# The output projection by pairs of tiles with seven part products, as the first part of the stream

## The chip, the cores and the metric

The kernel runs on one core of a Trainium2 chip. The metric is the device time of one execution in microseconds (us), the median of several runs. The core has a matmul engine (PE, with its weight loads, PEld), a vector engine (DVE), a scalar engine (ACT), a small general engine (POOL), and queues that move data between its memories (DMA); all DMA of this kernel is issued by the sync engine (SP). Each engine works through its instructions in program order and waits at an instruction until what it needs is there.

## The reference

One layer of an encoder over 2048 tokens of width 1024, all in f32:

```
xn = rms_norm(x, ln_mix_g)
proj = xn @ w_in
y_a = mlstm_group(proj[...])              # bidirectional, 4 heads x 128
y_b = mla_group(proj[...])                # attention, 4 heads x 128
h = x + concat([y_a, y_b]) @ w_out        # the output projection, 1024 x 1024
h = h + conv_gated_mlp(rms_norm(h, ln_ffn_g), w_up, conv_w, conv_b, w_down)
gate = sigmoid(rms_norm(h, ple_norm_g) @ w_ple_gate)
h = h + gate * rms_norm(p @ w_ple_proj, ple_post_g)
return rms_norm(h, final_g)
```

## The kernel before

**Split matmuls.** Each f32 operand is split into a high part (ACT casts it) and a low part (DVE subtracts the high part from it); a product is three matmul passes, low x high, high x low, high x high. The helper `split` does this, on lines 118 and 121 of the profile (120 and 123 after the change), for all parts of the kernel, so the tile's name tells them apart: `pt` are the transposed weights of attention, `wo` the weights of the projection, `yhl` its input, `op` the operands of the stream's right side and `fw`/`fwd` those of its left side.

**Stages.** The input projection; then attention with the mLSTM work beside it (a string of letters, `order`, gives what each of 64 attention tiles (head, 128 queries) issues, and at each "." in it `pump` issues a share of the mLSTM steps, which `SIDE` sets); then `out_proj`; then `up_down`, called the stream below.

**The output projection.** For each of 16 token tiles: `load_y` loads the tile's y, DVE scales its attention half by the softmax sums (`rb`), `split`; two halves of 512 columns, each 8 k-parts x 3 passes = 24 matmuls of 128x512 (`out_mm`, PE line 131, into `bk`); DVE adds the result to x (line 1143); the sum is stored (`h1_d`), squared on ACT (1064), turned into a factor on POOL (139, 141) and scaled in place by DVE (1066). The eight transposes of a tile (1075) stand one tile late, and ACT copies them to a tile that is stored to `x2_d`. The weights are loaded as eight `wor` and split to `wo0`..`wo7`, four of them beside the last attention head.

**The stream.** Products of matrices of 2x2 blocks by seven part products instead of eight. A pair is two tiles of 128 rows; for each, `prod` issues four k-parts x 3 passes = 12 matmuls into one of four banks (x and y in `fxy`, z in `fz`, and a spare one `fs`), in the order A11 x B11, S1 x T1, A22 x T4 of the pair before, S2 x T2, A12 x B21, S4 x B22 of the pair before, S3 x T3. S1 to S4 are sums of the left side, formed by DVE in `up_prep` one pair ahead. B.. are blocks of the right side and T1 to T4 sums of them; `sums`, `wsums` and `gsums` form the T ahead of time and store them, and `load_op` loads and splits a block's operands, four pieces of 128x512 for each of seven operands, through a ring of raw places (tags t0, t1, ...; `orot`). The first block of 22 pairs does the up projection of the first half of the tokens with x2 as its right side; then come the other half, three blocks of the down projection, and the gate. In the stream before, the first up block's B11, T1 and T2 are formed in place by `sums` inside `out_proj`, its other operands are loaded in pairs 0 and 1, and these two pairs take results over by other additions ("not seeded").

**Tile places.** Every tile has a place named by a tag (w0.., x0.., t0.., u0..). A new tile in a place waits until all readers of the old one are done. PSUM banks come from pools: `sc` (scores, also `bk`), `tr`, `pv`, `ml` up to the projection, `fa` and `fb` for the stream.

Of the kernel before, what the change touches and what calls it, by code (L numbers as in the profile page):

```python
# [10 lines left out]
F32 = mybir.dt.float32  # L11
# [26 lines left out]
SIDE = 617  # L38
# [22 lines left out]
class Block:  # L61
# [4 lines left out]
    def __init__(self, ctx, tc, d):  # L66
# [13 lines left out]
        self.gt = self.cst.tile([P, 16, 16], F32, name="gt")  # L80
        dt = self.dram.tile
# [14 lines left out]
        self.x2_d = dt([P, KT, S], F32, name="x2_d")  # L96
        self.t_d = dt([2, 4, P, 4, 512], F32, name="t_d")
# [50 lines left out]
    def run(self, out):  # L148
# [807 lines left out]
    def attend(self, side):  # L956
# [58 lines left out]
        cur, self.wo = self.first, []  # L1015
        pts, pend = [], None
        for i, (h, qt) in enumerate(seq):
# [35 lines left out]
            cur = nxt  # L1053
        pv(pend, 1)
        sums(1)
        for _ in side:
            pass


    def norm_load(self, h, g, ssq_junk):  # L1060

        nc = self.nc
        ssq = self.stat(1, "nt_s")
        nc.scalar.activation(ssq_junk, h, AF.Square, accum_out=ssq)
# [3 lines left out]
    def transpose_out(self, xn, otag, dst):
        nc = self.nc
        pt = (self.tbank(), self.tbank())  # L1070
        xo = self.at(otag, [P, KT, P], name="nt_o")
        for f in range(2):
            for j in range(4):
                kt = f * 4 + j
                nc.tensor.transpose(pt[f][:, j, :], xn[:, kt * P:(kt + 1) * P], self.ident)
            nc.scalar.copy(xo[:, f * 4:f * 4 + 4], pt[f])
        nc.sync.dma_start(dst, xo)

    def load_wo(self, k):
        nc = self.nc  # L1080
        raw = self.at(("w13", "w13", "w13", "w13", "w13", "w12", "u2", "w0")[k], [P, D], name="wor")
        nc.sync.dma_start(raw, self.d["w_out"][0, k * P:(k + 1) * P, :] if k < 4 else self.wo_d[k - 4])
        w = self.at(f"x{(0, 1, 2, 3, 6, 7, 4, 5)[k]}", [P, 2, D], F32R, f"wo{k}")
        self.split(raw, w[:, 0], w[:, 1])
        self.wo.append(w)

    def load_y(self, c):
        yr = self.at(f"w{5 + c % 2}", [P, 8, P], name="yr")
        self.nc.sync.dma_start(yr, self.y_d[c])
        rb = self.row_bcast(self.at(f"u{c % 2}", [P, 512], name="rb"), self.ri_d[c].rearrange("h t -> (h t)"), 512)  # L1090
        ya = yr[:, 4:8].rearrange("p h t -> p (h t)")
        self.nc.vector.tensor_tensor(ya, ya, rb, op=ALU.mult)
        if c:
            y = self.at(f"x{10 + c % 2}", [P, 2, 8, P], F32R, "yhl")
            self.split(yr, y[:, 0], y[:, 1])
            return y[:, :, 0:4], y[:, :, 4:8]
        ys = []
        for f in range(2):
            ys.append(self.at(("w4", "w9")[f], [P, 2, 4, P], F32R, "yhl"))
            self.split(yr[:, 4 * f:4 * f + 4], ys[f][:, 0], ys[f][:, 1])  # L1100
        return ys
# [776 lines left out]
```

## Time and profile before

| | us |
|---|---|
| median of 3 runs | 2957.03 (2951.71 to 2958.16) |
| the profiled execution | 2961.99, of which span 2960.2 |
| PE busy | 2895.7 (98% of the span), 14738 matmuls and transposes |
| weight loads (PEld) busy | 2437.3 (82%) |
| DVE busy | 1991.5 (67%) |
| ACT busy | 1476.6 (50%) |
| last score matmul of attention ends | 1226.4 |
| first matmul of the stream | 1443.8 |

The span is the time from the first to the last instruction on the core. Busy times overlap between engines. The projection lies between the two last rows, some 217 us.

### The profile page before, as it was taken

The page shows a single profiled execution, that of the slowest core. Times are in us where ns is not written, and L with a number is a line of the kernel's source. Part 1 is how long each engine was busy: PE and PEld are TensorE (multiplying, and loading weights), DVE is VectorE, ACT ScalarE, POOL GpSimd, SP SyncE. Part 2 cuts the span into 40 slices and gives each one's busy share as a digit, 9 for nine tenths or more (in the row PEclk, how much of TensorE's full clock was granted, in tenths as well). Part 3 has the DMA queues.
Part 4 walks back from the last instruction along what each step waited for, and adds up shares of the span by engine and source line. Part 5 has one row for each costly group of instructions (what it writes and reads, how often), then busy time and mean ns, then how long its engine had stood idle before and what let it go on. Part 6 is the DMA issues. An engine that isn't in the chain of part 4 may idle for free.

```text
span 2960.2 us, 40962 instructions
## 1 busy us (share of the span) xinstructions
PE 2895.7 (98%) x14738; PEld 2437.3 (82%) x14738; DVE 1991.5 (67%) x3677; ACT 1476.6 (50%) x2883; POOL 145.9 (5%) x278
## 2 busy tenths in 40 slices
PE   8999999999999999999999999999999999999998
PEld 7888888888888888888788888788887788878776
DVE  7521555777777777635677877767777767676776
ACT  7311544656665666523455555655556333244654
POOL 3100000000000000000000000000000000001111
PEclk9999999999999999999999999999999999999999
DMA  6612444443333333457734554657776757585864
GB/s 186 128 57 95 146 132 153 120 146 98 103 100 100 98 118 114 145 178 256 243 137 164 190 172 147 206 177 234 233 228 201 231 180 246 167 261 196 277 195 157
DMA packets 396253, 496.93 MB, mean 168 GB/s; under 512 B 32385, under 2 KB 265361, under 8 KB 396049
## 3 DMA queue, kind: packets, MB, share of 16 engines
q1 hardware_dynamic: 396048, 494.31, 52.4%
q8 instruction: 116, 1.90, 0.3%
q14 instruction: 89, 0.72, 0.1%
HBM read 318.39 MB, written 175.83 MB: 167 GB/s over the span
## 4 chain that ended last, share of the span: by engine, by line
PE 46%; DMA 4%; DVE 4%; issue 2%; ACT 2%; POOL 1%; SPq 0%; POOLq 0%; ACTq 0%; DVEq 0%
PE fxy L1427 30%; PE fz L1427 11%; PE bk L131 4%; PE fs L131 1%; DMA tsum<-x_d 1%; DMA opr<-tw_d 1%; DMA opr<-in_w_ple_gate 1%; DVE pj L1756 0%; DVE fw L121 0%; ACT junk L1770 0%; DMA opr<-t_d 0%; DVE hb L1757 0%; ACT fw L118 0%; DMA t_d<-tsum 0%; ACT op L118 0%
## 5 line engine op out<-in xcount | busy, mean ns | idle before, releaser
L1427 PE MATMUL fxy<-op,fw 128*128 128x512 f32 x3552 | 857.7, 393 | 15.3 <-DVE fh L1413 5.4
L1427 PEld LDWEIGHTS fxy<-op,fw 128*128 128x128 f32 x3552 | 662.6, 189 | 174.2 <-ACT ug L1580 13.6
L1427 PE MATMUL fz<-op,fw 128*128 128x512 f32 x1776 | 440.0, 390 | 3.2 <-DVE xt L1143 2.1
L1427 PEld LDWEIGHTS fz<-op,fw 128*128 128x128 f32 x1776 | 332.0, 188 | 72.4 <-DVE xt L1143 2.4
L131 PE MATMUL bk<-wsp,xh 128*128 128x512 f32 (+1 forms) x768 | 234.5, 386 | 0.0
L118 ACT CAST pt<-tb 128x512 fp32r<-128x512 f32 x256 | 147.1, 587 | 174.9 <-PE tb L972 174.2
L914 DVE TENSOR_REDUCE mx<-bk 128x1 f32<-128x512 f32 x256 | 175.2, 685 | 65.8 <-PE bk L913 61.6
L1427 PE MATMUL fxy<-op,fwd 128*128 128x512 f32 x888 | 215.3, 390 | 0.2 <-DVE fh L1413 0.2
L131 PE MATMUL ppv<-pt,kv 128*128 128x256 f32 x1536 | 203.9, 287 | 0.0
L121 DVE TENSOR_TENSOR pt<-tb,pt 128x512 fp32r<-128x512 f32 x256 | 174.2, 686 | 38.0 <-ACT pt L118 36.6
L1427 PEld LDWEIGHTS fxy<-op,fwd 128*128 128x128 f32 x888 | 165.9, 188 | 35.3 <-DVE fh L1413 1.0
L932 ACT ACTIVATE pe<-bk,nm 128x512 f32<-128x512 f32 x256 | 174.6, 696 | 32.8 <-DVE nm L926 27.1
L131 PEld LDWEIGHTS ppv<-pt,kv 128*128 128x128 f32 x1536 | 189.0, 191 | 0.5 <-ACT pt L118 0.4
L131 PE MATMUL bk<-wo,yhl 128*128 128x512 f32 x744 | 177.1, 396 | 5.2 <-DVE yhl L121 5.2
L131 PEld LDWEIGHTS bk<-wo,yhl 128*128 128x128 f32 x744 | 139.9, 190 | 34.3 <-DVE yhl L121 5.6
L131 PEld LDWEIGHTS bk<-wsp,xh 128*128 128x128 f32 x768 | 145.6, 190 | 25.2
L131 PE MATMUL bk<-wsp,xl 128*128 128x512 f32 (+1 forms) x384 | 150.9, 393 | 8.1 <-DVE xl L121 8.1
L131 PE MATMUL bk<-xh,wqk 128*128 128x512 f32 x480 | 157.4, 393 | 0.0
L972 PE MATMUL tb<-ident,pe 128*128 128x128 f32 x1024 | 150.0, 273 | 3.7 <-DVE pt L121 3.7
L972 PEld LDWEIGHTS tb<-ident,pe 128*128 128x128 f32 x1024 | 121.9, 140 | 22.6 <-DVE pt L121 5.3
L118 ACT CAST fw<-hraw 128x1024 fp32r<-128x1024 f32 (+1 forms) x72 | 70.2, 981 | 125.5 <-PE fxy L1427 96.3
L121 DVE TENSOR_TENSOR fw<-fwr,fw 128x1024 fp32r<-128x1024 f32 x88 | 107.4, 1221 | 31.7 <-ACT fw L118 31.7
(348 smaller groups left out, 4806.9 us busy)
## 6 DMA issues: line engine op xcount, KB each, us to landing
fwr<-in_w_up SPq DMA_DIRECT2D x66, 512.0 KB, 4.7
fh<-h_d SPq DMA_DIRECT2D x48, 512.0 KB, 4.2
h_d<-fh SPq DMA_DIRECT2D x48, 512.0 KB, 4.0
s_d<-fwr SPq DMA_DIRECT2D x44, 512.0 KB, 2.6
fws<-s_d SPq DMA_DIRECT2D x44, 512.0 KB, 4.0
rw<-row_d SPq DMA_DIRECT2D x32, 512.0 KB, 4.9
tw_d<-tsum SPq DMA_DIRECT2D x60, 256.0 KB, 5.1
opr<-tw_d SPq DMA_DIRECT2D x60, 256.0 KB, 5.2
```

Of the source, the lines that this page charges most:

```text
L118: nc.scalar.copy(hi, src)
L121: (sub or nc.vector).tensor_tensor(lo, src, _f(hi), op=ALU.subtract)
L131: mm = lambda *a, **k: self.nc.tensor.matmul(*a, **k, skip_group_check=more)
L914: nc.vector.tensor_reduce(s.mx[:, kb:kb + 1], ps, axis=AX.X, op=ALU.max)
L932: nc.scalar.activation(s.pe[:, kb % 2], s.banks[kb], AF.Exp, bias=s.nm, scale=ASCALE, accum_out=s.rs[:, kb:kb + 1])
L972: nc.tensor.transpose(t[:, j, :], s.p[kb][:, j * P:(j + 1) * P], self.ident)
L1427: nc.tensor.matmul(out, a[:, k * P:(k + 1) * P], parts[lo], start=first, stop=lo == 1 and k == last, skip_group_check=more)
```

## The change

The output projection becomes eight pairs, numbered -8 to -1, at the head of the stream, with w_out as the right side and y as the left. Its weights' four sums per k-part are formed by `osums` beside attention (tiles 6 to 21) and stored to `to_d`. At the end of attention, all seven operands of the new block are loaded by `load_op(0, ...)`, with four raw places (`RAWS`). `up_prep` is cut in two (`prep_a`, `prep_b`) so that pair -8 can be prepared in two steps; the mLSTM steps end three tiles before attention's end. The class `Out` loads y (w12, w13, one buffer) and x, stores the result, and does the norm and the transposes of the tiles between products of later pairs. `sums(0)` now stores all four sums, and the first up block's operands are loaded at pair -1 as those of every other block. In the last pair of the gate stage, S4 x B22 of the pair before comes earlier. `out_proj`, `load_wo`, `load_y`, `out_mm`, `norm_load`, `transpose_out` and `turn` are gone. The rest of the diff renumbers blocks and gives tiles other places.

```
-SIDE = 617
+SIDE = 668
...
         self.attend(tail(self.mlstm()))
-        self.out_proj()
+        left.close()
+        pools(left, "left", ("fa", 2))
         right.close()
-        pools(right, "right", ("fa", 2))
-        left.close()
-        pools(left, "left", ("fb", 2))
-        self.up_down(out)
+        pools(right, "right", ("fb", 2))
+        self.stream(out)
...
         for i, (h, qt) in enumerate(seq):
-            if h == NH - 1 and qt in (4, 6, 8, 10):
-                self.load_wo(qt // 2 - 2)
+            if 6 <= i < 22 and i % 2 == 0:
+                next(osums)
...
-            if i == len(seq) - 2:
-                self.y0 = self.load_y(0)
+            if i == last - 3:
+                for _ in side:
+                    pass
+                self.load_op(0, "B11")
+                o.load(-8)
+            if i == last - 2:
+                self.load_op(0, "T1")
+                self.prep_a(-8)
+                o.load_x(-8, 0)
...
-            if nxt is None:
-                self.ps0 = self.pml.tile([P, 512], F32, name="wo0", tag="ml")
-                self.out_mm(self.ps0, self.y0, range(4), slice(0, 512))
...
+            if i == last - 1:
+                for n in ("T2", "B21", "T3"):
+                    self.load_op(0, n)
+                    if n == "T2":
+                        self.prep_b(-8)
         pv(pend, 1)
         sums(1)
-        for _ in side:
-            pass
+        self.load_op(0, "T4")
+        self.load_op(0, "B22")
...
+    def osums(self):
+        tt = self.nc.vector.tensor_tensor
+        L, H = slice(0, SB), slice(SB, 2 * SB)
+        for k in range(4):
+            a, b = [self.at(f"u{i}", [P, D], name="wos") for i in range(2)]
+            self.nc.sync.dma_start(a, self.d["w_out"][0, k * P:(k + 1) * P, :])
+            self.nc.sync.dma_start(b, self.wo_d[k])
+            yield
+            tt(a[:, H], a[:, H], a[:, L], op=ALU.subtract)
+            tt(b[:, H], b[:, H], a[:, H], op=ALU.subtract)
+            tt(a[:, L], b[:, H], a[:, L], op=ALU.subtract)
+            tt(b[:, L], b[:, L], b[:, H], op=ALU.subtract)
+            for i, t in enumerate((a[:, H], b[:, H], a[:, L], b[:, L])):
+                self.nc.sync.dma_start(self.to_d[i, :, k], t)
+            yield
...
+    RAWS = {(0, "B11"): range(4), (1, "B11"): (0, 1, 2, 3, 6, 7), (1, "T4"): range(4), (2, "B11"): range(6),
+            (4, "B11"): range(8), (6, "B11"): (0, 1, 2, 3, 4, 5, 7), (6, "T4"): (0, 1, 3)}
...
+    BLOCKS = ((-8, 8, 4), (0, NC2, 4), (NC2, NC2, 4), (2 * NC2, 8, 4), (2 * NC2 + 8, 8, 4), (2 * NC2 + 16, 8, 3),
...
+class Out:
...
+    def done(self, s, e):
+        b, nc, t = self.b, self.nc, s.o[e]
+        nc.sync.dma_start(b.h1_d[2 * s.pr + e], t)
+        ssq = b.stat(2, "nt_s")
+        for f in range(2):
+            nc.scalar.activation(b.at("s2", [P, SB], BF16, "junk"), t[:, f * SB:f * SB + SB], AF.Square,
+                                 accum_out=ssq[:, f:f + 1])
+        s1 = b.stat(1, "nt_t")
+        nc.gpsimd.tensor_tensor(s1, ssq[:, 0:1], ssq[:, 1:2], op=ALU.add)
+        self.norm[2 * s.pr + e] = t, b.rsq(s1, 1, 1.0 / D)
...
+    def beside(self, s, at, bank):
...
+        c = 2 * i + 12 if at < 4 else 2 * i + 15
+        if at in (1, 2, 5, 6) and 0 <= c < NT:
+            self.turn(c, at - 1 if at < 4 else at - 5, bank)
+        c = 2 * i + 15 if at == 4 else 2 * i + 14
+        if at in (4, 7) and 0 <= c < NT:
+            self.scaled(c)
...
+        if (i, at) == (-3, 3):
+            self.sums = b.sums(0)
+        if (i, at) in ((-3, 4), (-3, 6), (-3, 7), (-2, 2), (-2, 3), (-2, 5), (-2, 6), (-1, 1)):
+            next(self.sums)
...
-            if prev:
+            if prev and i < n - 1:
                 rest_z(prev)
```

The first place is the end of attention on ACT. `pe` are the exponentials of a tile (four banks), `pt` the casts of its transposes, `ya` a copy of its result. Before, from the first exponential of the last tile on, with `hy` of the mLSTM and the projection's first operands:

```order
L932 ACTIVATE pe,rs<-bk,nm 128x512
L118 CAST pt<-tb 128x4x128 x2
L932 ACTIVATE pe,rs<-bk,nm 128x512 x2
L868 ACTIVATE hy,dsq<-hy 128x128 x2
L988 COPY ya<-ppv 128x256
L932 ACTIVATE pe,rs<-bk,nm 128x512
L118 CAST yhl<-yr 128x512
L118 CAST pt<-tb 128x4x128
L868 ACTIVATE hy,dsq<-hy 128x128
L118 CAST pt<-tb 128x4x128
L118 CAST wo_13226<-wor 128x1024
L868 ACTIVATE hy,dsq<-hy 128x128
```

The same place after:

```order
L120 CAST fwd<-yr 128x512
L120 CAST op<-opr 128x512
L933 ACTIVATE pe,rs<-bk,nm 128x512
L120 CAST op<-opr 128x512
L989 COPY ya<-ppv 128x256
L120 CAST op<-opr 128x512 x2
L933 ACTIVATE pe,rs<-bk,nm 128x512 x2
L120 CAST op<-opr 128x512
L120 CAST pt<-tb 128x4x128
L933 ACTIVATE pe,rs<-bk,nm 128x512
L120 CAST pt<-tb 128x4x128
L120 CAST op<-opr 128x512 x2
```

The casts `op<-opr` of the new block's operands now stand between the four exponentials and between the casts of the transposes; before, these places held `hy` pieces and splits of `wo`.

The second place is the start of the projection, on DVE, from the splits of the last tile's transposes to the first addition of a product to x (`xt`). Before:

```order
L121 TENSOR_TENSOR pt<-tb,pt 128x4x128 x2
L121 TENSOR_TENSOR wo_13226<-wor,wo_13226 128x1024
L871 SCALAR_TENSOR_TENSOR hy<-hy,rsr,og 128x128 x4
L121 TENSOR_TENSOR wo_13231<-wor,wo_13231 128x1024
L121 TENSOR_TENSOR pt<-tb,pt 128x4x128 x2
L1092 TENSOR_TENSOR yr<-yr,rb 128x512
L121 TENSOR_TENSOR wo_13236<-wor,wo_13236 128x1024
L1467 MEMSET uv 128x2
L121 TENSOR_TENSOR wo_13241<-wor,wo_13241 128x1024
L121 TENSOR_TENSOR yhl<-yr,yhl 128x1024
L1511 TENSOR_SCALAR gt<-gt 128x8
L1143 TENSOR_TENSOR xt<-xt,wo_13099 128x512
```

The same place after, with the first addition on line 1346 (the S2 result of pair -8):

```order
L123 TENSOR_TENSOR pt<-tb,pt 128x4x128
L123 TENSOR_TENSOR op<-opr,op 128x512 x2
L123 TENSOR_TENSOR pt<-tb,pt 128x4x128 x2
L123 TENSOR_TENSOR op<-opr,op 128x512 x4
L123 TENSOR_TENSOR fw_13463<-yr,fw_13463 128x1024
L123 TENSOR_TENSOR op<-opr,op 128x512 x3
L123 TENSOR_TENSOR fw_13455<-yr,fw_13455 128x1024
L123 TENSOR_TENSOR op<-opr,op 128x512
L1336 TENSOR_TENSOR yr<-yr 128x512
L123 TENSOR_TENSOR op<-opr,op 128x512 x3
L1436 TENSOR_SCALAR gt<-gt 128x8
L1346 TENSOR_TENSOR xt<-xt,fxy 128x512
```

The first addition stands behind eleven more operand splits and two splits of pair -7 (`fw`). On PE the products of that stretch stand so after the change; `fw_12988` and `fw_12989` hold A11 and A12 of pair -8, `fw_12997`/`fw_12998` S1, `fw_13218`/`fw_13219` S2, and `fw_13455` A11 of pair -7:

```order
L1011 MATMUL tb<-ident,gt 32x128
L1361 MATMUL fxy<-op,fw_12989 128x512 x3
L1361 MATMUL fxy<-op,fw_12988 128x512 x4
L1361 MATMUL fz<-op,fw_12997 128x512 x4
L1361 MATMUL fz<-op,fw_12998 128x512 x4
L1361 MATMUL fz<-op,fw_12997 128x512 x4
L1361 MATMUL fxy<-op,fw_13218 128x512 x4
L1361 MATMUL fxy<-op,fw_13219 128x512 x4
L1361 MATMUL fxy<-op,fw_13218 128x512 x4
L1361 MATMUL fxy<-op,fw_13455 128x512 x10
L1361 MATMUL fxy<-op,fw_12988 128x512 x4
L1361 MATMUL fxy<-op,fw_12989 128x512 x4
```

A12 x B21 (the second row group of `fw_12988`) comes ten matmuls behind S2 x T2, with no other work of pair -8 between them; before, PE had the rest of tile 0's part products there.

The third place is the middle of the projection on DVE. Before, one tile and the next (line 1092 is the scaling of y, 1143 the addition, 1066 the norm's scaling):

```order
L1092 TENSOR_TENSOR yr<-yr,rb 128x512
L1143 TENSOR_TENSOR xt<-xt,bk 128x512 x2
L121 TENSOR_TENSOR yhl<-yr,yhl 128x1024
L1066 SCALAR_TENSOR_TENSOR xt<-xt,rsr,g_13246 128x1024
L1092 TENSOR_TENSOR yr<-yr,rb 128x512
L1143 TENSOR_TENSOR xt<-xt,bk 128x512 x2
L121 TENSOR_TENSOR yhl<-yr,yhl 128x1024
L1066 SCALAR_TENSOR_TENSOR xt<-xt,rsr,g_13246 128x1024
```

After, half a pair, from the addition of A12 x B21's result (1582 is the scaling of y, 1346 an addition, 1610 the norm's scaling in two halves):

```order
L1346 TENSOR_TENSOR xt<-xt,fxy 128x512
L123 TENSOR_TENSOR fw_13782<-yr,fw_13781 128x1024
L1346 TENSOR_TENSOR xt<-xt,fz 128x512
L123 TENSOR_TENSOR fw_13776<-yr,fw_13775 128x1024
L1346 TENSOR_TENSOR xt<-xt,fxy 128x512
L1582 TENSOR_TENSOR yr<-yr,rb 128x512
L1346 TENSOR_TENSOR xt<-xt,fz 128x512
L1610 SCALAR_TENSOR_TENSOR xt<-xt,rsr,g_13414 128x512
L1610 SCALAR_TENSOR_TENSOR xt<-xt,rsr,g_13416 128x512
L123 TENSOR_TENSOR fw_13956<-yr,fw_13955 128x1024
```

The scaling of a y that has just been loaded now stands ahead of the norm's scaling of the even tile of the pair before, whose transposes follow in the next pair.

## Rows read from the trace of the kernel before

**Rows 1.** The page: busy time, share of the span, instructions, by engine.

```profile
PE 2895.7 (98%) x14738; PEld 2437.3 (82%) x14738; DVE 1991.5 (67%) x3677; ACT 1476.6 (50%) x2883; POOL 145.9 (5%) x278
```

**Rows 2.** PE's waits (total us, times, longest) in 520:1230 and in 1520:2960.

```profile
PE tb L972 <- DVE pt L121: 3.7, 11, 0.5
...
PE fxy L1427 <- DVE fh L1413: 5.5, 5, 2.1
PE fxy L1427 <- ACT c L1576: 5.1, 6, 1.9
PE fxy L1427 <- ACT ug L1580: 4.8, 2, 2.6
```

**Rows 3.** PE's timeline: start, us, instructions, [idle before <- what ended it].

```profile
1226.01 0.40 PE L913 MATMUL bk<-kv,q_s 128*128 128x512 f32 x1
...
1237.71 5.88 PE L131 MATMUL ppv<-pt,kv 128*128 128x256 f32 x47
...
1247.82 0.66 PE L876 MATMUL mb<-ident,hy 128*128 128x128 f32 x4 [0.40 <-DVE xt L1143]
...
1257.13 13.66 PE L131 MATMUL bk<-wo,yhl 128*128 128x512 f32 x48 [5.21 <-DVE yhl L121]
...
1417.07 1.06 PE L1075 MATMUL tb<-ident,xt 128*128 128x128 f32 x8 [2.65 <-DVE xt L1066]
...
1443.83 2.79 PE L1427 MATMUL fz<-op,fw 128*128 128x512 f32 x11 [2.14 <-DVE xt L1143]
```

**Rows 4.** The chain that ended last, in 1225:1300: start, us, what.

```profile
1271.66 10.90 PE bk L131 x48
1282.56 0.87 PE tb L1075 x8
```

**Rows 5.** Windows: busy us (instructions) of each engine, granted clock, DMA share, GB/s.

```profile
520.00:1226.00 706.00, 691.92 (x4685) 621.67 (x4684) 515.83 (x1336) 431.28 (x1161) 44.54 (x62) 1.00 0.35 109
...
1250.00:1260.00 10.00, 4.79 (x16) 3.56 (x15) 4.50 (x5) 2.08 (x3) 0.74 (x2) 0.78 0.83 274
```

**Rows 6.** The chain that ended last, behind PE's last product.

```profile
2950.58 0.74 DVE pj L1756
```

**Rows 7.** Tile opr: the two instructions of a split, ns min/median/max.

```profile
L118 ACT CAST op<-opr x137: 602/618/628, 1436.1 to 2787.4; 128x512 fp32r<-128x512 f32 x137
L121 DVE TENSOR_TENSOR op<-opr,op x137: 682/686/694, 1436.7 to 2789.0; 128x512 fp32r<-128x512 f32 x137
```

**Rows 8.** Operand loads (line 1302) in 1400:1470, then ACT's and DVE's timeline there.

```profile
DMA to landing us min/median/max: 4.3/4.5/5.8
...
1441.84 1.20 ACT L118 CAST op<-opr 128x512 fp32r<-128x512 f32 x2 [2.52 <-DMA opr<-t_d]
...
1436.75 3.70 DVE L121 TENSOR_TENSOR op<-opr,op 128x512 fp32r<-128x512 f32 x6 [0.65 <-ACT op L118]
```

**Rows 9.** Instructions by line in 2360:2580: busy us, mean ns | idle before.

```profile
L121 DVE TENSOR_TENSOR fw<-hraw,fw 128x1024 fp32r<-128x1024 f32 x33 | 40.2, 1222 | 4.0 <-ACT fw L118 4.0
```

**Rows 10.** DVE's timeline at the start of the projection.

```profile
1252.40 0.69 DVE L1092 TENSOR_TENSOR yr<-yr,rb 128x512 f32<-128x512 f32 x1 [4.65 <-DMA yr<-y_d]
```

**Rows 11.** Instructions by line in 1257:1440, the projection's norm.

```profile
L1066 DVE SCALAR_TENSOR_TENSOR xt<-xt,rsr,g 128x1024 f32<-128x1024 f32 x15 | 19.3, 1284 | 21.0 <-DMA h_d<-xt 21.0
...
L1064 ACT ACTIVATE junk<-xt 128x1024 bf16<-128x1024 f32 x14 | 14.8, 1056 | 5.2 <-DVE xt L1143 3.5 <-issue 1.6
...
L141 POOL TENSOR_TENSOR rsr<-rsm,nhalf 128x1 f32<-128x1 f32 x14 | 7.6, 541 | 1.2
```

**Rows 12.** Loads of y (line 1089) in 1240:1440.

```profile
DMA to landing us min/median/max: 3.9/4.1/4.3
```

More of the change, by code (lines that the diff above doesn't have):

```diff
@@ L1068, in transpose_out @@
[L1068 to L1101, printed above, removed]
@@ L1193, in sums @@
     def sums(self, b):
[L1196 removed]
         t0 = b * 2 * SB
[L1198 to L1200 removed]
         for k in range(4):
             src = lambda i: self.x2_d[:, k + i // 2 * 4, t0 + i % 2 * SB:t0 + i % 2 * SB + SB]
[L1203 removed]
+            yield from self.sum4(src, lambda i: self.t_d[b, i, :, k])
@@ L1433, in rest_y @@
             prod(s.y, s.ops["A22"], "T4", True)
-            if s.down:
+            if s.acc:
                 add(s.o[1][:, L], s.o[1][:, L], s.y)
+                if s.out:
+                    first.done(s, 1)
+                    return
                 nc.sync.dma_start(self.h2_d[2 * s.pr + 1], s.o[1])
@@ L1440, in rest_y @@
                 gate.part(s, 1, 0, s.y)
-            elif s.seeded:
+            else:
                 nc.scalar.copy(s.uv[:, 2:2 + SB], s.y)
-            else:
-                add(s.uv[:, 2:2 + SB], s.p1, s.y)
         def rest_z(s):
             prod(s.z, s.ops["S4"], "B22", True)
-            if s.down:
+            if s.acc:
                 add(s.o[0][:, H], s.o[0][:, H], s.z)
+                if s.out:
+                    first.done(s, 0)
+                    return
                 nc.sync.dma_start(self.h2_d[2 * s.pr], s.o[0])
@@ L1520, in up_down @@
         NG = NUP + 24
-        for i in range(n):
+        for i in range(blocks[0][0], n):
             blk = max(q for q, bl in enumerate(blocks) if bl[0] <= i)
@@ L1530, in side @@
             def side(at):
-                gate.beside(s, at, prev.spare if at % 2 and prev else s.spare)
+                bank = prev.spare if at % 2 and prev else s.spare
+                first.beside(s, at, bank)
+                gate.beside(s, at, bank)
             s = Pair()
             s.i, s.ops, s.pr = i, self.ops.pop(i), j
-            s.up, s.down, s.gate = i < NUP, NUP <= i < NG, i >= NG
+            s.out, s.up, s.down, s.gate = i < 0, 0 <= i < NUP, NUP <= i < NG, i >= NG
+            s.acc = s.out or s.down
             s.h, s.done, s.sq = [], [0, 0], {}
@@ L1540, in up_down @@
             s.z, s.spare = [self.pfb.tile([P, SB], F32, name=t, tag=t) for t in ("fz", "fs")]
-            s.seeded = i > 1
             prod(x, s.ops["A11"], "B11")
-            if s.seeded:
-                nc.scalar.copy(s.y, x)
-            else:
-                s.p1 = self.at(f"t{6 + i}", [P, SB], name="p1")
-                nc.scalar.copy(s.p1, x)
-            if s.down:
-                s.o = outs.pop(i)
-            if i == 0:
-                load(0, "B21")
+            nc.scalar.copy(s.y, x)
+            if s.acc:
+                s.o = first.tiles if s.out else outs.pop(i)
             load(then, "B11")
@@ L1556, in up_down @@
             prod(s.z, s.ops["S1"], "T1")
-            if s.seeded and not s.down:
+            if not s.acc:
                 s.p5 = self.at("t4" if s.gate else f"t{6 + i % 2}", [P, SB], name="p5")
@@ L1637, in up_down @@
                     next(steps[i])
-            if i == 0:
-                load(0, "T4")
-                load(0, "B22")
             load(then, "B21")
```

330 lines of the change are left out of this document (160 added, 170 removed).

## The prediction

> **What bounds the kernel now.** The page's busy times come first [rows 1]: the matmul engine, PE, is busy 98% of the span and DVE 67%, so time is won by giving PE fewer matmuls or by ending one of its waits, and other work costs something only where PE comes to wait for it. Next are PE's waits by what ended them. Attention has small ones (the largest kind 3.7 us in 11 pieces), and the stream from 1520 us on has three kinds worth 15.4 us together [rows 2]; the stream changes operands five times in that stretch, so 3.1 us a change. The rest lies at the two ends of the output projection. PE's own timeline shows them [rows 3]: after the last score matmul (1226.01 + 0.40, called T0 below) PE works on until the part products of tile 0 run out, waits 0.40 and then 5.21 us, and takes 13.66 us for 48 matmuls; at the far end it waits 2.65 and 2.14 us. The chain that ended last gives the plain price: 48 matmuls in 10.90 us, 8 transposes in 0.87 [rows 4], so 0.227 us a matmul, one behind the other with no gap. In the stretch with the wait the granted clock was 0.78, over attention 1.00 [rows 5]: the 48 matmuls behind the wait took 13.66 - 10.90 = 2.8 us more because the clock had gone, after 5.2 us of idleness, from its level of 2.4 GHz to 1.2 GHz for a while.
>
> **Matmuls removed.** Before, 16 tiles x 48 = 768; after, 8 pairs x 7 products x 12 = 672. 96 x 0.228 = **-21.9 us**. The 128 transposes stay, eight to a tile. The saving is whole where PE sets the pace, and the row of 48 without a gap shows that for the middle of the projection [rows 4].
>
> The Trainium skill, Perfetto Trace Analysis, section Identifying the Most-Contended Engine, holds against such a reading that the busy share of matmuls says little of how near the roofline a kernel is, since they are pipelined, and that the share of weight loads should be read. That share is 82% [rows 1]; priced by it the 96 matmuls would save 18 us and the forecast would be 4 us higher. The trace shows no idle time inside the row of 48, so the sum keeps 21.9.
>
> **Waits removed.** The start of the old projection goes with its code: 0.40 + 5.21 + 2.8 = **-8.4 us**. At the far end 2.65 + 2.14 = **-4.8 us** goes [rows 3]. The order of the gate stage's last quarters changes too; the chain behind PE's last product has pieces of 0.74 us [rows 6], of which one or two may go: **-1 us** (bounds 0 and -2).
>
> **What the start costs instead.** Pair -8 needs 28 operand pieces, seven operands of four, each one a load, an ACT cast (0.618) and a DVE subtraction (0.686) [rows 7]. B11 and T1 are asked for two to three tiles before the end of attention, T2, B21 and T3 behind the order of the last tile but one, T4 and B22 after the last. They share four raw places, so a load can leave only when the fourth piece before it has been subtracted. The nearest loads are those of the first up pair: 4.3 to 5.8 us to landing, median 4.5, and a cast waited 2.52 us for one [rows 8]. One turn of four takes 4.5 + 0.62 + 0.69, near 6 us. The casts stand in program order on ACT, between the exponentials of attention's last tile and the casts of its transposes. T2's pieces are done about T0 + 5, once the first exponentials are out. Four turns follow (B21, T3, T4, B22): T0 + 29. Pieces of other kinds stand between them (two splits of 1.22 [rows 9], two copies): T0 + 32. Then comes DVE's addition of the first S2 result (0.69), which stands behind B22's last piece; PE's A12 x B21 writes the tile that this addition reads, waits for it, and ends at T0 + 36. Without a wait PE would get there after 24 transposes (2.6 us) and 72 value matmuls (47 take 5.7 [rows 3], so 8.8) of attention, three products of 12 and ten matmuls of pair -7 (10.5) and A12 x B21 (2.7): T0 + 25. The loss is **+11 us**. A landing of 3.5 us would make it 7; one of 5.5 us, with the queues as full as in the old start (274 GB/s [rows 5]), 18. That the last exponential stands behind B21's first piece is inside the same 11 us, since PE passes all of it in order. The lower clock behind such a wait is priced as the old one was: **+2.8 us** (bounds 0 and 5).
>
> **The pairs.** DVE has per pair of the projection two row scalings and four sums (6 x 0.69), three splits of 1.22 and one of 0.69, six additions (4.1) and two norms (2 x 1.28): 15.2 us of 84 x 0.228 + 16 transposes (1.75) = 20.9, one pair ahead of PE. One chain has little room. Counted from the end of A12 x B21 of a pair, the first transpose of the even tile of the pair before comes after 8 + 12 + 12 + 1 matmuls and 8 transposes, 8.4 us. The scaling of that tile stands in DVE's queue behind the scaling of the next y, whose load can leave only when DVE has split the last piece of the y before it (one buffer): 0.7 + 1.2, then 4.1 for the landing [rows 12], 0.6, an addition 0.6 and the scaling 1.2: 8.4 us. So no wait or a small one: **+3 us** for eight pairs (bounds 0 and 12, a landing 1.5 us later).
>
> **Projection to up.** All 28 pieces of the first up block are loaded at pair -1, beside the preparation of pair 0 and the norms: 19.2 us of subtractions and another 14 of a pair's work, 33 us of DVE work around one 20.9 us pair. Before, six raw pieces were split at once in 3.70 us [rows 8] and the others beside the first two pairs. Five such changes in the stream cost 3.1 us each [rows 2]; with the norms on top **+4 us** (bounds 1 and 10).
>
> **Beside attention.** The sums of the weights are 16 subtractions of 0.69 (11 us of DVE), 8 loads of 512 KB and 16 stores. DVE was busy 516 of 706 us there [rows 5], so they fit, except that a subtraction that waits for its load holds the in-order queue, and with it the maxima behind which PE's next tile stands. In exchange the eight splits of w_out (1.22 each) go. The mLSTM work is spread more densely (668 steps for 617) and ends three tiles early, when ACT and DVE take on the first pair's pieces. **+3 us** together (bounds -1 and 10); PE's largest wait of this kind was 3.7 us in 11 pieces [rows 2].
>
> **Sum.** -21.9 - 8.4 - 4.8 - 1 + 11 + 2.8 + 3 + 4 + 3 = -12.3. The profiled run took 2961.99 us (span 2960.2), 5 us above the median of 2957.03 of the runs shown; the sum is made of stretches of that run and applied to the median: **2945 us**.
>
> **Rivals.** (a) *The new start is short.* If the loads land in 3.5 us and ACT runs ahead, the wait is 4 us and the clock hardly falls: 11 + 2.8 becomes 5, and the time 2936. For it: attention moves only 109 GB/s [rows 5], little to fight over. Against it: in the old start DVE waited 4.65 us for one y [rows 10], and the four places are a plain ring. (b) *Start and attention are heavier.* 18 us of wait, 5 of clock and 8 in attention add 7 + 2.2 + 5 = 14: 2959, no change. For it: 16 operand loads, a y and an x crowd the queue at once. (c) *The norm chain holds PE in every pair* (the other sign). The even tile has no room in my count. Its landing could be later, and the norm before it longer: squares (half of 1.06 twice), POOL (0.54 and more), and DVE's scaling waited 21.0 us in all, over 15 tiles, for the store of the tile that it overwrites [rows 11]. If PE waits 1.4 us for each of 16 tiles, 22.4 instead of 3, the sum is +7: 2964. It decides from (12.3 + 3 + 5.9) / 16 = 1.3 us a tile. Against it: the odd tile has 1 us more room, and y landed in 3.9 to 4.3 us throughout [rows 12]. (d) *The projection was not bound by PE*, so that fewer matmuls give nothing: excluded but for its ends by the row of 48.
>
> **How the numbers follow.** The likeliest, a sum of -6 to -19 as the start's wait goes from 18 to 5 us, 0.43, its own range 2938 to 2951. (a) 0.25, (b) 0.19, (c) 0.13. About 0.2% (5.9 us) is what a measurement of this kernel can tell from no change: below 2951.1 faster, above 2962.9 slower. (a) and the likeliest lie below: faster 0.68; (b) and a little of (c): same 0.20; the rest slower, 0.12. The range reaches from (a) with an easy change to the up projection, 2930, to the lower end of (c), 2963.
>
> **What would show it.** PE's busy time down by about 22 us; on PE's timeline waits of 7 to 18 us in the first pair, ended by DVE's addition, and a granted clock below 0.9 behind them; none above 1 us between products in pairs -7 to -2; some 4 us around the first up pair; PE's waits in attention within 5 us of before. The prediction would be wrong with a wait of 2 us or more in each pair that ends with the DVE scaling (rival c), with waits in attention's early tiles ended by a sum of weights, or with a start under 5 us (rival a), which would put the time below 2938.

## The result: as slow as before or a little slower

The changed kernel takes **2963.63 us** (median of 8 runs, 2961.75 to 2966.63), the kernel before 2958.94 beside it (8 runs, 2951.71 to 2960.8): ratio **1.0021, 95% interval 1.0012 to 1.003**. The forecast was 2945 us, with a range up to 2963. The profiled execution took 2963.16, span 2961.2, against 2960.2 before; the profiled run of before lay 3 us above its median, that of after on it, so the spans differ by 1.0 us and the medians by 4.7.

The page of the changed kernel, busy times to hold against [rows 1]:

```profile
PE 2886.7 (97%) x14642; PEld 2418.6 (82%) x14642; DVE 2053.0 (69%) x3786; ACT 1512.5 (51%) x2964; POOL 156.5 (5%) x294
```

The 96 matmuls are gone, but PE's busy time fell by 9.0 us, not by 22. A busy row is no measure of work where PE is held up in small steps or runs at its lower clock: further down one reads 8 matmuls in 3.64 us, at a granted clock of 0.50 (1.2 GHz of 2.4), which take 1.8 at full clock. So the account below counts matmuls and transposes, prices them at what they take back to back (0.227 us for 128x512, as in [rows 4], 0.109 for a transpose; in attention 0.120 for 128x256 and 0.112 for 128x129, medians of the trace before), and calls the rest of a stretch's time lost. It compares the two profiled executions, so it explains the 1.0 us between their spans.

| us | before | after | difference | forecast |
|---|---|---|---|---|
| work of PE, whole kernel | | | -21.8 | -21.9 |
| lost: start to first score matmul | 17.1 | 15.3 | -1.8 | 0 |
| lost: attention, first to last score matmul | 31.0 | 38.6 | +7.5 | +3 |
| lost: old projection and change to up, to A22 x T4 of pair 2 at 1502.65 | 16.7 | | -16.7 | -13.2 |
| lost: new start, last score to A22 x T4 at 1272.78 | | 8.2 | +8.2 | +13.8 |
| lost: six pairs, 1272.78 to 1408.26 | | 9.9 | +9.9 | +3 |
| lost: change to up, 1408.26 to 1505.61 | | 17.6 | +17.6 | +4 |
| lost: from A22 x T4 of pair 2 to the end | | | -2.0 | -1 |
| sum | | | +1.0 | -12.3 |

The stretches of the stream run from one row of 12 matmuls `fxy<-op,fwd` (A22 x T4, once a pair) to another. The first row of losses is scatter: the first score matmul comes at 497.3 to 499.9 us in the changed kernel and in runs that leave all before it alone. PE's timeline of the changed kernel at the new start; it answers to [rows 3]:

```profile
1233.98 0.40 PE L914 MATMUL bk<-kv,q_s 128*128 128x512 f32 x1
...
1240.63 0.66 PE L973 MATMUL tb<-ident,pe 128*128 128x128 f32 x4 [1.84 <-ACT pe L933]
1243.30 0.57 PE L133 MATMUL ppv<-pt,kv 128*128 128x256 f32 x1 [2.01 <-ACT pt L120]
...
1263.86 3.47 PE L1361 MATMUL fxy<-op,fw 128*128 128x512 f32 x14 [1.51 <-DVE xt L1346]
```

The wait for DVE's addition that the prediction priced at 11 us is there, and is 1.51 us; ACT's late exponential and cast cost 1.84 and 2.01. Further on, from pair -1 into the up pairs:

```profile
1408.26 3.01 PE L1361 MATMUL fxy<-op,fwd 128*128 128x512 f32 x12
...
1424.50 0.73 PE L1361 MATMUL fxy<-op,fw 128*128 128x512 f32 x2 [1.65 <-ACT op L120]
...
1430.24 0.49 PE L1361 MATMUL fz<-op,fw 128*128 128x512 f32 x1 [1.73 <-ACT op L120]
1430.89 3.64 PE L1361 MATMUL fz<-op,fw 128*128 128x512 f32 x8 [0.15 <-ACT op L120]
...
1435.44 3.00 PE L1361 MATMUL fxy<-op,fwd 128*128 128x512 f32 x12
...
1446.48 1.53 PE L1361 MATMUL fxy<-op,fw 128*128 128x512 f32 x3 [1.73 <-ACT ug L1500]
...
1463.71 2.88 PE L1361 MATMUL fxy<-op,fwd 128*128 128x512 f32 x12
...
1490.48 3.02 PE L1361 MATMUL fxy<-op,fwd 128*128 128x512 f32 x12
```

From one A22 x T4 to the next these hold 19.9, 20.8 and 24.3 us of work (84 matmuls with 8 and with 16 transposes, then 103 matmuls with 8) and take 27.2, 28.3 and 26.8, so 14.7 of the 17.6 us are lost in the first two. PE stands idle for 9.4 us of the change (the sum of its waits): 4.4 for casts of operand pieces (`op`), 2.5 for copies to `ug`, which ACT makes in the same queue as those casts, the rest for DVE and one cast of a left side. Twice the granted clock fell to 0.50 for 3.4 us, the first time in the row of 3.64 us; that costs some 3 us more (half of 6.8, an estimate). Windows of the same stretch (columns: length, PE, PEld, DVE, ACT, POOL, granted clock, DMA share, GB/s), with one from attention ahead and that row behind:

```profile
540.00:600.00 60.00, 58.00 (x386) 51.41 (x385) 48.29 (x119) 31.62 (x77) 0.00 (x0) 1.00 0.76 244
1385.00:1408.00 23.00, 21.64 (x102) 17.12 (x101) 18.02 (x27) 7.91 (x16) 3.24 (x6) 1.00 0.94 313
1408.00:1435.00 27.00, 22.80 (x93) 17.26 (x92) 19.61 (x28) 12.80 (x23) 3.13 (x6) 0.94 0.94 297
1435.00:1464.00 29.00, 24.72 (x108) 18.91 (x107) 19.09 (x29) 19.43 (x39) 2.81 (x6) 0.94 0.87 290
1464.00:1490.00 26.00, 24.91 (x110) 19.17 (x109) 20.66 (x29) 16.39 (x24) 0.00 (x0) 1.00 0.93 305
...
1431.10:1434.30 3.20, 3.20 (x8) 2.38 (x8) 3.13 (x5) 0.00 (x0) 0.00 (x0) 0.50 0.96 301
```

Beside PE no compute engine is full there, DVE is at 66 to 79%. What is near full is DMA: 0.87 to 0.94 of 16 engines' time, near 300 GB/s, for 105 us. That alone does not hold PE, though. In a later change of operands, to a block of the down projection, the same trace has more and PE loses nothing (102 matmuls of 0.227 us in 23.00):

```profile
2439.00:2462.00 23.00, 23.00 (x102) 18.78 (x101) 21.50 (x33) 12.82 (x21) 0.00 (x0) 1.00 0.99 350
```

The account of 1385:1490:

```profile
DMA packets 26886, 31.56 MB, mean 301 GB/s; under 512 B 1392, under 2 KB 17786, under 8 KB 26879
```

And what SP issued there (the queue of all transfers; idle before in this queue is not waiting of PE):

```profile
1407.63 1.75 SPq L1154 DMA_DIRECT2D tsum<-x_d  x4
...
1412.62 4.40 SPq L1164 DMA_DIRECT2D t_d<-tsum  x4
1418.04 2.30 SPq L1225 DMA_DIRECT2D opr<-x_d  x4
1420.39 0.90 SPq L1225 DMA_DIRECT2D opr<-t_d  x2
```

The sums of the up projection's right side (`tsum`) run as four batches through the raw places t0 to t3. The last is loaded at 1407.6 and stored at 1412.6; only then may the first operands of the new block (`opr<-x_d`, B11) use the places, at 1418.0 (SP waits there 1.8 us in four pieces for `t_d<-tsum` to land), and PE, which stands idle for them from 1422.85, gets the first at 1424.5.

### The profile page after: what moved, and what is told of

Same layout as the page of the kernel before. It is cut to its first block, busy times and chain, and to the rows that moved or that the text cites. A ratio compares the mean times of both kernels' runs of the same rounds, so it can differ in the third digit from the quotient of the medians.

```text
span 2961.2 us, 41131 instructions
## 1 busy us (share of the span) xinstructions
PE 2886.7 (97%) x14642; PEld 2418.6 (82%) x14642; DVE 2053.0 (69%) x3786; ACT 1512.5 (51%) x2964; POOL 156.5 (5%) x294
## 4 chain that ended last, share of the span: by engine, by line
PE 77%; DVE 7%; DMA 5%; ACT 5%; issue 4%; POOL 1%; SPq 0%; POOLq 0%; ACTq 0%; DVEq 0%
PE fxy L1361 30%; PE bk L133 13%; PE fz L1361 12%; PE ppv L133 4%; PE tb L973 3%; PE bk L910 1%; PE bk L912 1%; PE bk L911 1%; PE bk L913 1%; PE bk L914 1%; PE fs L133 1%; PE gb L133 1%; ACT pe L933 1%; PE mb L848 1%; DVE fw L123 1%
## 5 line engine op out<-in xcount | busy, mean ns | idle before, releaser
L1361 PE MATMUL fxy<-op,fw 128*128 128x512 f32 x3936 | 953.5, 393 | 20.0 <-DVE fh L1346 5.5
L1361 PEld LDWEIGHTS fxy<-op,fw 128*128 128x128 f32 x3936 | 731.9, 188 | 197.4 <-ACT ug L1500 13.9
L1361 PE MATMUL fz<-op,fw 128*128 128x512 f32 x1968 | 493.0, 392 | 6.0 <-DVE fh L1346 2.3
L1361 PEld LDWEIGHTS fz<-op,fw 128*128 128x128 f32 x1968 | 368.6, 188 | 83.5 <-ACT op L120 5.3
L1361 PE MATMUL fxy<-op,fwd 128*128 128x512 f32 x984 | 239.9, 392 | 0.4 <-DVE p L1346 0.3
L1361 PEld LDWEIGHTS fxy<-op,fwd 128*128 128x128 f32 x984 | 184.1, 189 | 39.7 <-DVE p L1346 0.8
L123 DVE TENSOR_TENSOR pt<-tb,pt 128x512 fp32r<-128x512 f32 x256 | 174.1, 683 | 31.6 <-ACT pt L120 30.7
L973 PEld LDWEIGHTS tb<-ident,pe 128*128 128x128 f32 x1024 | 122.6, 141 | 27.2 <-DVE pt L123 7.0
L120 ACT CAST fw<-hraw 128x1024 fp32r<-128x1024 f32 (+1 forms) x72 | 70.2, 981 | 125.2 <-PE fxy L1361 96.2
L1346 DVE TENSOR_TENSOR fh<-fh,fxy 128x512 f32<-128x512 f32 x95 | 65.1, 685 | 92.0 <-PE fxy L1361 91.6
L123 DVE TENSOR_TENSOR op<-opr,op 128x512 fp32r<-128x512 f32 x177 | 114.8, 685 | 18.7 <-ACT op L120 18.4
L120 ACT CAST op<-opr 128x512 fp32r<-128x512 f32 x177 | 104.3, 619 | 44.5 <-PE fxy L1361 19.1
```

The source lines that it names most:

```text
L120: nc.scalar.copy(hi, src)
L123: (sub or nc.vector).tensor_tensor(lo, src, _f(hi), op=ALU.subtract)
L973: nc.tensor.transpose(t[:, j, :], s.p[kb][:, j * P:(j + 1) * P], self.ident)
L1346: add = lambda o, a, b: tt(o, a, b, op=ALU.add)
L1361: nc.tensor.matmul(out, a[:, k * P:(k + 1) * P], parts[lo], start=first, stop=lo == 1 and k == last, skip_group_check=more)
```

## The experiments

Most kernels were run once, and one time is too coarse for parts of a few us (the kernel before had medians of 2959.66 to 2961.32 beside them). So the verdicts go by stretches of the trace: tiles 0 to 13 of attention (changed kernel 165.65 us, before 157.6), the rest of attention (571.0), the new start (38.80), the six pairs (135.5; 125.6 is work) and the change to up (97.35; 79.8 is work). Where an expectation counts the change by products, it ends it one pair sooner (77.7 us). Runs whose edit lies elsewhere show the scatter: new start 38.3 to 40.2, pairs 134.0 to 136.7, change to up 96.2 to 98.4, tiles 0 to 13 165.2 to 167.3, the rest of attention 570.4 to 571.1.

**Attention: sums of weights, and density.** e1 forms no sums of the weights:

```
-            if 6 <= i < 22 and i % 2 == 0:
-                next(osums)
...
-                src = self.to_d if blk == 0 else ...
+                src = self.d["w_out"][0, k * P:(k + 1) * P, 0:SB] if blk == 0 else ...
```

> Leaves out the sums of the weights beside attention (16 subtractions, 8 loads, 16 stores); T1 to T4 of the first block are loaded from w_out itself. Attention, from the first to the last score matmul, takes 736.7 us with the change and 726.9 before; of this difference some 2 us is mLSTM work of PE that now lies ahead of the last score, and 7.5 us is lost time, most of it in tiles 2 to 13. Theory: the sums' loads and stores and their place in DVE's queue cost PE 5 to 7 us there, so attention takes 730 to 732 us. Rival: the denser mLSTM work (668 steps for 617) costs it, and attention stays at 735 us or more.

Tiles 0 to 13 took 160.74, the rest 569.8; one run 2960.18. The sums cost some 5 to 6 us. But attention was not back at the loss of before (tiles 0 to 13 lost 9.1, before 7.7, after 14.0). e6 keeps the sums and spreads the mLSTM as before (`SIDE = 617`):

> The mLSTM work spread as before (617 for 668), so that some 50 steps are left at the point three tiles before the end where they are all issued at once. Theory, the sums of the weights are what costs attention: tiles 0 to 13 stay at 165 to 166 us and the tiles behind them at 569 to 572, or a little longer for the bunch. Rival, the denser work costs it: tiles 0 to 13 fall by 2 us or more.

Tiles 0 to 13 fell to 159.75 (9.9 lost), with the sums there; but the steps left over at the end stood in a bunch, the rest took 587.35, with single waits of 5.8 and 4.1 us, and the run 2977.72. So neither alone costs the early tiles much; together they do. e8 and e10 write the sums at tiles 26 on. e8 changes only the loop:

```
-            if 6 <= i < 22 and i % 2 == 0:
+            if 26 <= i < 42 and i % 2 == 0:
```

> The sums of the weights at tiles 26 to 41 of attention instead of 6 to 21, where the queues move 100 GB/s and not 240. Theory: the 5 us that they cost come from the transfers at the start of attention, so attention takes 731 to 733 us instead of 736.7 and the kernel 4 to 5 us less, 2959 to 2960. Rival: their place in DVE's in-order queue costs it wherever they stand, and attention stays at 735 us or more, the time at 2963.

It tests nothing: the first subtraction ran at 533.3 us, where it had run at 532.6, so the written place does not decide where these instructions stand: in the changed kernel, too, the subtractions run from 532.6 to 587 us, in tiles 2 to 7, and not in the 6 to 21 of its code (2967.57, ratio 1.0023, 1.001 to 1.0035). In e10 data holds them: a column of a result of that tile is copied into both tiles ahead of their loads.

```
+            for t in (a, b):
+                self.nc.vector.tensor_copy(t[:, 0:1], self.hold)
```

> The weights' sums are held back by data: a column of each place is first written with a maximum of attention tile 26, 28, ..., so loads and subtractions really stand there (in the run before, with another loop index alone, they stood where they had stood, from 533 us on). Theory, the 5 us are the coincidence of these transfers and subtractions with the busy start of attention: tiles 0 to 13 take 160 to 162 us instead of 165.7, and tiles 14 to 63 stay within 1.5 us of 571.0. Rival, the sums cost it anywhere: tiles 14 to 63 get 4 us longer.

Tiles 0 to 13 took 160.69, as without sums, the rest 572.76, 1.75 more; one run 2957.8. Its window, against the row of the changed kernel above:

```profile
540.00:600.00 60.00, 60.00 (x408) 54.17 (x408) 44.78 (x112) 33.12 (x79) 0.00 (x0) 1.00 0.42 134
```

The same window of the kernel before:

```profile
540.00:600.00 60.00, 59.87 (x402) 53.81 (x401) 44.03 (x109) 33.46 (x80) 0.00 (x0) 1.00 0.42 122
```

PE is full again there. From the first to the last score matmul attention took 736.65 in the changed kernel, 733.45 in e10 and 730.58 without sums (e1). So of the 6 us that the sums cost, half is where they stand; 2.9 stay where they are made late.

**The start.** e5 gives the first B11 six raw places, not four (`(0, "B11"): range(6)`):

> Six raw places instead of four for the first block's operands at the end of attention. From the last score matmul to the A22 product in pair -7 the changed kernel takes 38.8 us, of which 30.6 is work of PE and 5.4 are waits. Theory: the ring of four sets the pace of the operands, so with six the stretch takes 35 to 36 us. Rival: casts in ACT's order behind the exponentials and the queue's own pace set it, and it stays within 1 us of 38.8. In both cases the change of operands to the up projection, full of transfers, may take back what is won.

The start took 39.93, no shorter than in the other runs; one run 2966.74. The ring of four, on which the prediction built its 11 us, is not what sets it.

**The pairs.** e4 puts the transposes of the even tile one product later:

```
-        if at in (1, 2, 5, 6) and 0 <= c < NT:
-            self.turn(c, at - 1 if at < 4 else at - 5, bank)
+        if at in (2, 3, 5, 6) and 0 <= c < NT:
+            self.turn(c, at - 2 if at < 4 else at - 5, bank)
```

> The transposes of the even tile stand one product later (behind S1 x T1 and A22 x T4 of the pair before instead of behind A11 x B11 and S1 x T1). Theory: they wait for the norm's scaling, 0.8 to 1.3 us a pair, so the stretch from the A22 product in pair -7 to that in pair -1, now 135.5 us, takes 129 to 131 us, and the kernel 5 us less, 2959. Rival: what is late is DVE's queue as a whole (loads of y), so the wait shows up at the next product, the stretch stays at 134 us or more and the time at 2963.

The pairs took 129.98, 5.5 less. In the changed kernel PE waited at the even tile's transposes in each of the six, 0.3 to 1.3 us and 5.9 in all; for two of them the profile names DVE's scaling, for the others other releasers:

```profile
1314.07 0.63 PE L1620 MATMUL fs<-ident,xt 128*128 128x128 f32 x4 [1.15 <-DVE xt L1610]
...
1338.19 0.63 PE L1620 MATMUL fs<-ident,xt 128*128 128x128 f32 x4 [1.32 <-DVE xt L1610]
```

The kernel did not gain: 2965.6 (10 runs), ratio 1.0019 (1.001 to 1.0029) to the kernel before. The change to up took 101.3, 4 us more. SP's queue and the clock say why:

```profile
1405.50 1.80 SPq L1154 DMA_DIRECT2D tsum<-x_d  x4
...
1416.46 1.92 SPq L1225 DMA_DIRECT2D opr<-x_d  x4
```

PE reaches pair -1 4.7 us earlier (A22 x T4 at 1403.54), the operands leave 1.6 us earlier. It waits 2.64 us for the first instead of 1.65, and the granted clock is 0.50 for 17 us of the change, not 6.8, with as much idle time of PE in all (9.3 for 9.4). So what was won ahead of this place was lost in it, in good part as lower clock. e1 and e8, too, have 13.7 us of it, at 97.5 and 98.4 us, so it does not add up one to one.

**The change to up: what is left out makes it short.** e2 splits the block's 28 pieces from a tile on the chip and loads none; e3 forms and loads no sums for it; e7 does not store tiles 10 to 15 of h1 (3 MB).

```
+            if blk == 1:
+                self.split(self.o.g2[k % 2], hi, lo)
+                continue
```

> The 28 operand pieces of the first up block are split on ACT and DVE as before, but from a row tile that is on the chip, with no load (the right side of that block is left out). From the A22 product in pair -1 to the one in pair 2 the changed kernel takes 77.7 us, of which 60.7 is work of PE. Theory: transfers are the limit there (DMA share 0.94), so without these 7 MB the stretch takes 66 us or less. Rival: the casts and subtractions of 28 pieces beside the preparation of pair 0 are the limit, and it stays at 74 us or more.

```
-        if (i, at) == (-3, 3):
-            self.sums = b.sums(0)
-        if (i, at) in ((-3, 4), (-3, 6), ...):
-            next(self.sums)
```

> Leaves out the four sums of the up projection's input in pairs -3 to -1 (16 loads, 16 subtractions, 16 stores of 256 KB); the first up block's T1 to T4 are loaded from the sums of w_out. Operand loads and splits stay. Theory, transfers are the limit: the same stretch of 77.7 us takes about 70 (half of the loss goes, since 8 MB of some 20 do). Rival, work on ACT and DVE is the limit: 75 us or more, since only 4 of the 16 subtractions lie in it.

```
-        nc.sync.dma_start(b.h1_d[2 * s.pr + e], t)
+        if 2 * s.pr + e < 10:
+            nc.sync.dma_start(b.h1_d[2 * s.pr + e], t)
```

> The projection's result is not stored for tiles 10 to 15 (the down projection reads x there instead): 3 MB less to move in pairs -3 to 0, while all operand loads, their ring of raw places and all work on ACT and DVE stay. From the A22 product of 1408.26 to the one of 1505.61 the changed kernel takes 97.4 us (79.8 of it work). Theory, the bytes in flight are the limit (300 GB/s): 3 MB are 10 us, of which 5 to 9 are won there, so 88 to 92 us. Rival, the ring of raw places or the order of the issues is the limit: 95 us or more.

From 1408 on the change took 83.96 in e2 (one run 2951.67), 87.2 in e3 (2957.03) and 90.5 in e7 (2961.10), instead of 97.35. The windows of the change, in the order changed kernel, e2, e3, e7:

```profile
1408.26:1505.61 97.35, 87.78 (x371) 67.36 (x370) 73.82 (x102) 58.41 (x98) 5.94 (x12) 0.96 0.84 272
1408.60:1492.56 83.96, 82.05 (x377) 66.64 (x376) 70.92 (x102) 55.21 (x94) 9.89 (x12) 1.00 0.74 239
1409.46:1496.66 87.20, 81.97 (x371) 65.67 (x370) 66.97 (x93) 53.68 (x92) 5.94 (x12) 1.00 0.80 253
1411.48:1501.96 90.48, 83.29 (x372) 65.37 (x370) 72.11 (x103) 55.77 (x96) 4.41 (x12) 1.00 0.83 266
```

The granted clock does not fall in e2, e3 and e7, so up to 3 us of each gain may be clock. e7 also spares DVE's scaling a wait for the stores of the tiles that it overwrites (1.7 us), but PE's waits for that scaling hardly changed (1.9 and 1.5 us). In e2 all 28 casts and subtractions are still made, beside the norms, so it was not their 33 us of DVE work that was too much. DMA was as full as before for a while (0.95, 313 GB/s in 1409:1431); PE stood idle for 1.9 us in all, and never for a cast of an operand piece. A22 x T4 of the next pairs:

```profile
1430.92 2.88 PE L1364 MATMUL fxy<-op,fwd 128*128 128x512 f32 x12
...
1473.44 2.88 PE L1364 MATMUL fxy<-op,fwd 128*128 128x512 f32 x12
```

**The change to up: bytes, data or places?** e9 moves 3 MB less, by work done twice: the S of pairs 0 to 2 are not stored, but formed again when the block is read a second time.

```
-        if 0 <= i < NC2:
+        if 3 <= i < NC2:
             nc.sync.dma_start(self.s_d[i, ...
```

> The sums S1 to S4 of the first three up pairs are not stored for the second half of the tokens; there these three pairs load the whole weights and form the sums again. 3 MB less to move in pairs -1 to 2, with every operand load, its ring and its splits in place, and nothing left out. Theory, bytes at 300 GB/s are the limit at the change: from the A22 product of 1408.26 to that of 1505.61 (97.4 us) it takes 88 to 93 us, and the kernel 5 to 8 us less, 2955 to 2959, less up to 2 us for the added subtractions in pairs 22 to 24. Rival, the six stores lie behind what PE waits for: 95 us or more.

The change took 93.85, 3.5 us less, between what the two sides had named, with the granted clock at 0.96 as in the changed kernel; pairs 22 to 24, which form them again, lost nothing that can be told; one run 2962.84. e12 forms and stores the sums, but the block reads other sums, made long before (`src = self.to_d if blk < 2`):

> The four sums of the up projection's input are formed and stored as in the changed kernel, with the same bytes in the same places, but the first up block reads its T1 to T4 from the sums of w_out, so no operand waits for the data of a sum. From the A22 product of 1408.26 to that of 1505.61 (97.4 us; 87.2 where the sums were left out). Theory A, the serial chain of sums by data: 90 us or less. Theory B, the raw places t0 to t3, which the last sums hold until their stores land, and the full queues: 95 us or more, since both stay.

The change took 100.1 (one run 2971.47), with a granted clock of 0.93 and no less idle time of PE: the operands do not wait for the sums' values. e13 takes them off the sums' places, B11 through t6 and t7:

```
-(1, "B11"): (0, 1, 2, 3, 6, 7),
+(1, "B11"): (6, 7), (1, "T1"): (0, 1, 2, 3, 6, 7),
```

> B11 of the first up block is loaded through two raw places of its own (t6, t7), so its first loads go out ahead of the stores of the last sums; the other operands use the ring as before. Nothing left out, same bytes. Theory B (places held by the last sums): B11 comes 5 us or more earlier and T1 has the whole ring, so the stretch takes 92 to 94 us instead of 97.4. Theory A or bytes alone: 96 us or more.

The change took 98.3 (one run 2966.02; granted clock 0.93), no gain. The windows of the change in e9, e12 and e13:

```profile
1410.37:1504.22 93.85, 87.62 (x374) 67.82 (x372) 71.61 (x100) 57.26 (x97) 5.09 (x12) 0.96 0.79 251
1409.55:1509.66 100.11, 90.47 (x372) 69.22 (x370) 73.64 (x102) 58.32 (x98) 5.60 (x12) 0.93 0.83 266
1409.36:1507.66 98.30, 89.64 (x371) 69.39 (x370) 73.62 (x102) 58.18 (x98) 5.75 (x12) 0.93 0.85 272
```

SP's queue in e13:

```profile
1411.34 0.90 SPq L1225 DMA_DIRECT2D opr<-x_d  x2
...
1418.77 0.94 SPq L1225 DMA_DIRECT2D opr<-x_d  x2
1419.76 2.24 SPq L1164 DMA_DIRECT2D t_d<-tsum  x4
1423.28 3.38 SPq L1225 DMA_DIRECT2D opr<-t_d  x4
```

Two loads leave 7 us sooner. The other two need t6 and t7 back, and the last sums' stores, which stand behind them in SP's order, leave 7 us later (1419.8 for 1412.6), and with them the loads of T1. The wait was handed on, so the run doesn't tell places from bytes.

**Together.** e11 is e4, e9 and e10 in one; e14 adds e13.

> The even tile's transposes one product later, the sums of three up pairs not stored, and the weights' sums held back to tile 26. If the change to the up projection was what took back the 5 us of the later transposes, these now count: 5 (attention) + 5 (pairs) + 5 to 8 (change) below the changed kernel's time, 2945 to 2950 where the kernel before takes 2959, so faster than both by 0.3%. If the change still fills up, the 5 us of the pairs are lost again: 2952 to 2955.

> As the run with three edits (even tile's transposes later, sums of three pairs not stored, the weights' sums held back), with B11's own raw places. That run took 95.8 us in the stretch and 2957.2 us. Theory B: 90 to 92 us and 2951 to 2954, faster than the kernel before (2960 beside it) by more than 0.2%. Theory A or bytes alone: 2956 to 2958 and no difference that can be told.

| | median us | before beside it | ratio, 95% | pairs | change to up |
|---|---|---|---|---|---|
| e11 | 2957.21 (11 runs) | 2961.01 (15) | 0.9994, 0.9984 to 1.0003 | 130.5 | 95.8 |
| e14 | 2955.83 (12 runs) | 2959.68 (17) | 0.9988, 0.9979 to 0.9997 | 130.6 | 93.8 |

Both fell short of what was expected. The gain in the pairs stays. Attention took 734.35 in e11, but 736.69 in e14, as long as in the changed kernel; why is open. The change to up still loses 14 to 16 us. e14 is faster than the kernel before, by a tenth of a per cent.

## Why the prediction was wrong

**The step that failed is "Projection to up".** Its term, +4 us with bounds of 1 and 10, measured 17.6. It priced DVE's 33 us of splits and took over the 3.1 us of the stream's other changes; it did not count what DMA has to carry, nor ask when the operand loads can leave. Beside the 28 pieces (7 MB) the ends of the projection (x, h1, x2), the last sums, the first weights of up and its S all move in these 105 us, 31.6 MB. Even at 350 GB/s, the rate of the row at 2439, they would take 90 us, an estimate, against 86 us of PE's work in that time (355 matmuls and 48 transposes). The kernel before gave only a hint of this: its change from projection to stream moved 28.4 MB in 110 us, with PE's waits of 2.65 and 2.14 us [rows 3] in it:

```profile
1360.00:1470.00 110.00, 104.56 (x491) 85.98 (x489) 72.57 (x100) 46.56 (x76) 5.91 (x14) 1.00 0.80 258
```

That these transfers are what makes the change long is shown by e2, e3, e7 and e9: each takes transfers out, and e2, e7 and e9 leave every cast and product of the stretch as it was; the change shortens by 13.4, 10.2, 6.9 and 3.5 us, beside a scatter of 2.2. That the queues are full is not enough, as the row at 2439 shows (share 0.99, PE not held). That the operands wait for the sums' data is ruled out by e12. How the 17.6 us divide between full queues and the order of places and stores in SP's queue stays open: e13, meant to tell, moved a wait and removed none.

The Trainium skill, Perfetto Trace Analysis, section DMA Optimizations, says that small transfers, below 2 KB, carry significant overhead each. The transfers of this stretch have 256 or 512 KB, but they go as packets, two thirds of them below 2 KB, and for packets the trace agrees: in 1385:1490 one of 512 B took 27 ns, one of 2048 B 84 and one of 4096 B 159 (medians), so some 8 ns a packet beside 0.037 ns a byte, an estimate from these three. No run here changes the packet size.

**Matmuls removed** held: -21.8 of work for -21.9 (a count, at the price of a row without a gap). "The saving is whole where PE sets the pace" is the half that did not hold: at the change PE does not set it alone, and e4 shows 5.5 us won in the pairs and 4 lost there.

**Waits removed** was right in kind and 3.5 us too small: the old projection lost 16.7, its small gaps and the first two up pairs included. **The tail** came as forecast: from the start of PE's last matmul to the end it is 12.5 us before and 11.4 after (11.2 to 11.9 in all other runs). The other microsecond of the -2.0 is within the scatter of that long stretch (1440 to 1448 us ahead of the last matmul).

**What the start costs**: 8.2 for 13.8. The mechanism was partly right (DVE's addition of the first S2 result holds A12 x B21, 1.51 us), the rest was a late exponential and a late cast on ACT, each some 2 us, and 3.4 us at the lower clock, which the prediction had looked for behind its wait. The turns of four that made 11 us are not what limits it (e5). By its own turns a landing of 5.5 us would have given 15 us of wait, not the 18 that it names and rival (b) uses.

**The pairs**: 9.9 for 3. Rival (c)'s mechanism was there: the even tile's transposes waited 0.3 to 1.3 us in a pair, twice by the profile for DVE's scaling, and moving them by a product gave 5.5 us back (e4). The count of 8.4 us against 8.4 saw that there was no room, and priced that at next to nothing. The odd tiles kept their room, so (c) in full, 1.4 us for each of 16 tiles, did not come.

**Beside attention**: 7.5 for 3, inside its bounds. PE's waits for splits of transposes hardly grew (4.2 us in 13 pieces, [rows 2] has 3.7 in 11); the loss is in tiles 0 to 13, where the sums' loads and stores meet the denser mLSTM (DMA 0.76 for 0.42, DVE 48.3 of 60 us for 44.0). e10 gets 5.0 us of it back there, and loses 1.75 later.

The time came out nearest rival (c)'s 2964. That is luck: (c) is in it with a part of 6.9 us, and the 13.6 us by which the change to up was missed stand in no rival.

## What to carry to other kernels

Before work is moved onto a stretch, sum the bytes that it will move and compare the time that they need at rates of the trace with the work of the fullest engine; here 90 us for 31.6 MB at 350 GB/s stood against 86 us of PE's work, so neither had room. The sum does not say how much will be lost: that also hangs on when each load can leave. Time saved ahead of such a stretch can be given back in it (e4), so repair that stretch first. A load that shares a place with the stores of another stage, or that stands in front of them in one queue, waits for them or makes them wait; look where the instruction really stands in the queue, not where the code writes it.

## What had not been expected of the hardware

A full stretch has no one rate: 290 to 313 GB/s at 0.87 to 0.95 around the change (in e2, without the operands' loads, 313 too), 350 at 0.99 in the row at 2439. Packets of 512 B carry 27% of the bytes in 1385:1490 and 13% in 2439:2462. The granted clock also falls behind waits that are short: at the new start, in a row of the windows of the changed kernel,

```profile
1243.00:1253.00 10.00, 9.70 (x63) 9.18 (x64) 7.97 (x15) 6.96 (x14) 0.00 (x0) 0.83 0.73 239
```

it was 0.83 with PE busy 9.70 of 10 us, a mean of 2.4 GHz and 3.4 us at 1.2 GHz, after two waits of 1.84 and 2.01 us; [rows 5] had 0.78 behind a wait of 5.21. At the change it fell twice, each time behind a wait of 1.73 us. So the granted clock can hide a loss in a row that looks busy.
